# Differential heads: keys and values by seven products over weight sums made in DRAM; the down projection's sums made later

## The chip, the core and the metric

The kernel runs on one core of a Trainium2 chip. TensorE (PE) multiplies, VectorE (DVE), ScalarE (ACT) and GpSimd (POOL) work on tiles in on-chip memory, SyncE (SP) and POOL issue DMAs, which 16 DMA engines carry out. Each engine takes its instructions in program order and waits on semaphores for the others. The metric is device time in microseconds (us), the median of several runs; before the change it is 971.36 us (three runs, 970.71 to 972.44).

## The reference, cut to what matters

One encoder layer on 512 tokens and 16 learned meta tokens (528 rows), model width 1024, in float32. Both attention branches have eight heads.

```
xn = rmsnorm(h)
proj = xn @ w_in                       # sb q|k|v, df q|k|v, 1024 columns each
o_sb = stick-breaking attention, 8 heads of width 128
s = einsum(dq, dk) * 64 ** -0.5        # df: two maps of width 64 per head
p = softmax(where(mask, s - slope * dist, -inf))
w = p[:, :, 0] - lam * p[:, :, 1]
o_df = rmsnorm(w @ dv, subln_g) * (1 - lam_init)
merged = g0 * (o_sb @ w_br_sb) + g1 * (o_df @ w_br_df)   # g = sigmoid(xn @ w_gate + b)
h = h + merged @ w_out
hn = rmsnorm(h)
h = h + (silu(hn @ w_ffn_gate) * (hn @ w_ffn_up)) @ w_ffn_down
y = rmsnorm(h)[16:]
```

## The kernel before

All float32 products are made of two parts: a value is split into a high part (ACT copies it to the PE's fp32r format, `wh`) and a rest (DVE subtracts, `wl`). `mm3` (L259) then issues three matmuls per 128-row slice of the inner dimension: hi*hi, hi*lo, lo*hi (L262, L263, L264). So each weight chunk of 512 KB (1024 x 128, eight slices `k`) goes through: a DMA by SP into a `wst` or `wsu` tile (L179), a cast on ACT and a subtraction on DVE (L77, L78, in `split`), then PE.

The weights come in the order of one list, `stream`. `prepare` runs a given number of chunks ahead of their use and issues loads, casts and splits; the constants STAGE = 5, READY = 3 and, for differential heads and later, 2 set how far.

The program goes: heads of the stick-breaking branch (`br` 0), heads of the differential branch (`br` 1), gates, output projection, feed-forward loop over 22 blocks f of 128 columns, down projection. In a head, PE works on head h's scores and outputs, and in between on `units` of head h+1's q, k and v projections and of the `y` projections of earlier heads; each `yield n` in `sb_head` and `df_head` lets n units run. The 528 rows are two halves of 264 (`HL`), so k and v are made in pieces of 264 columns; `xT_h` and `xT_l` are the split, transposed input.

Stick-breaking heads 2 to 7 make k and v together by seven block products instead of eight (Strassen-Winograd over two halves of the inner dimension, the two weight blocks v and k, and the two token halves). `seven_units` issues them; the weight sums that they need are made on DVE by `c1` to `c4` (L208, L209, L216, L223), the token sums once, in tiles `tA` and `tB`. The feed-forward loop does the same with its gate and up weights (`wst` and `wsu`). Differential heads make k and v plainly: 3 chunks, 8 slices each, `kv_units` for k and the like for v.

In `df_head` (h) DVE reduces the score tiles `z` with the bias to `pr` and their maxima (L676), ACT takes the exponential, DVE scales the two maps and combines them (L705, L706); four tiles t = 0 to 3, of 144 to 528 columns. PE then transposes `pr` (L528), and the outputs follow. `k_evac` splits k (L651, L652) and copies it to the other 64 partitions by a POOL DMA (L655); `q_evac` does it for q (L645). Odd heads keep q and k in a buffer of their own, `dqk`; the row blocks `y_out` of the y projections are added up in DRAM by POOL DMAs (L766, L768).

The down projection also uses seven products. Its weight sums `ds1` to `ds4` (the profile's `ds`) are made in DRAM by POOL DMAs: 24 copies, then 24 accumulating DMAs, 512 KB each but for the last block of each sum (256 KB). `sum_job` (L136 to L141) issues one; each waits for the last cast that ACT had been given, which paces it. Before the change one job is issued after every second unit of the heads, from 16 us to 393 us. After the gates only `hres` (L1044, four POOL DMAs of 512 KB, the residual input) and loads use the DMA engines.

In the gates POOL multiplies each gate by its y (L1036), DVE adds the two (L1037) and ACT casts the sum.

Of the kernel before, what the change touches and what calls it, by code (L numbers as in the profile page):

```python
# [9 lines left out]
F32 = mybir.dt.float32  # L10
# [30 lines left out]
def block_kernel(ctx: ExitStack, tc: tile.TileContext, x, meta, norm_mix_g, w_in, w_gate, b_gate,  # L41
# [46 lines left out]
    for h in range(NH):  # L88

        for i in (0, 1, 2) if h < SEVEN else (2, 1, 0):  # L90
            cols(("sb", h, i), w_in, i * D + h * P)
        if h > 2:
            rows(("y_sb", h - 3), w_br_sb, (h + 1) % 2 * 512, (h - 3) // 2 * 2)
    for h in range(NH):
        for i in range(3):
            cols(("df", h, i), w_in, (3 + i) * D + h * P)
        if h < 3:
            rows(("y_sb", h + 5), w_br_sb, (h + 1) % 2 * 512, (h + 5) // 2 * 2)
        else:
            rows(("y_df", h - 3), w_br_df, (h + 1) % 2 * 512, (h - 3) // 2 * 2)  # L100
# [17 lines left out]
    DK = range(0, NK, 2)  # L118
    sums_dram = ctx.enter_context(tc.tile_pool(name="sums_dram", bufs=1, space=bass.MemoryType.DRAM))
    w_sum = {(n, k0): sums_dram.tile([P, 2, 512], F32, name=f"d{n}_{k0}") for n in ("s1", "s2", "s3", "s4") for k0 in DK}  # L120
# [3 lines left out]
    for w, _, _ in DOWN:  # L124
        for k0 in DK:
# [3 lines left out]
            else:  # L129
                stream.append((("down", w, k0), w_sum[w, k0], 0, 512, 0, min(2, NK - k0)))  # L130

    def raw_down(w, k0):
        k, c0 = raw_at[w]
        return w_fd[:, k + k0:k + min(k0 + 2, NK), c0:c0 + 512]

    def sum_job(to, of, k0, add):  # L136
        src = raw_down(of, k0) if of in raw_at else w_sum[of, k0][:, 0:min(2, NK - k0)]
        dst = w_sum[to, k0][:, 0:min(2, NK - k0)]
        kw = dict(accum_op=ALU.add, max_dma_last_dim=2048) if add else {}
        paced = mybir.DependencyInfo(mybir.DependencyClass.Sync, mybir.DependencyReason.DATA)  # L140
        tc.add_manual_dep(nc.gpsimd.dma_start(dst, src, **kw).ins, cast["last"].ins.name, paced)  # L141

    background = [(to, of, k0, i > 3) for i, (to, of) in enumerate(
        (("s1", "a21"), ("s2", "a11"), ("s3", "a21"), ("s4", "a12"), ("s1", "a22"), ("s3", "a11"), ("s2", "s1"), ("s4", "s2")))
        for k0 in DK]

# [10 lines left out]
    def stage_one():  # L157
        n = len(staged)
        if n == len(stream):
            return False  # L160
        key, view, c0, cw, k0, k1 = stream[n]

        if n >= first_down + 3 and "slots" not in fpools:
            return False
        if key[0] == "fu" and key[1]:
            if "w" not in fpools:
                return False
            st = fpools["w"].tile([P, KT, P], F32, tag="wsu", bufs=2, name="wsu")
# [8 lines left out]
        staged.append(st)  # L177
        for a, b in ((0, 4), (4, 8)) if n < 2 else ((0, k1 - k0),):
            nc.sync.dma_start(st[:, a:b], view[:, k0 + a:k0 + b, c0:c0 + cw])  # L179
        return True  # L180
# [69 lines left out]
    def weights(key):  # L250
        at = at_of[key]
        if at < START:
            return loaded[key]
        if at >= first_ffn:
            return fpools["down"](key)
        prepare(prep_at[key] + (READY if at < at_of["df", 0, 0] else 2))
        return loaded[key]
# [144 lines left out]
    def seven_units(f, vT, k_neg):  # L402
# [5 lines left out]
        def run(w, t, i, start):  # L408
            prepare(prep_at[{"a": c1, "s": c2}[w[0]] if w in ("a11", "a12", "s1", "s2") else c4 if w == "s4" else c3, f] + READY)
            product(f, w, xsum[t], e[i], start)  # L410
# [33 lines left out]
    def kv_all(br, h, k_evac, d):  # L444
        vu, turn = v_units((br, h, 2), d)
        if sevens((br, h, 1)):
            return seven_units((br, h), d["vT"], k_evac), turn
# [180 lines left out]
    def df_units(h):  # L628
        d = {}
        hs = (slice(0, 64), slice(64, 128))  # L630
        if h % 2:

            both = opool.tile([P, 4 * L + 2 * SEQ], F32R, tag="y_df", name="dqk", bufs=1)
            q = [both[:, 4 * L + c * SEQ:4 * L + (c + 1) * SEQ] for c in range(2)]
            k = [both[:, 2 * c * L:2 * (c + 1) * L].rearrange("p (a l) -> p a l", a=2) for c in range(2)]
# [12 lines left out]
        def k_evac(ps, s, scale):  # L648
            for c in range(2):
# [99 lines left out]
    def y_units(name, i, o):  # L749

        def unit(fs):
            wh, wl = weights((name, i))
            for f in fs:
                ps = mm_tile()
                cs = slice(f % 4 * P, (f % 4 + 1) * P)
                mm3(ps, [(wh[:, k, cs], wl[:, k, cs], o[0][:, k], o[1][:, k]) for k in range(2)])
                if y_out:
                    ys = y_out[0][:, y_count[0] % KT]
                elif y_count[0] % 2:
# [268 lines left out]
    for f in range(KT):  # L1028
# [135 lines left out]
    with tc.tile_pool(name="ffn", bufs=1) as fp:  # L1164
# [102 lines left out]
        for f in range(1, NFF):  # L1267
# [152 lines left out]
```

## Time and profile before

| what | value |
|---|---|
| median of three runs | 971.36 us (970.71 to 972.44) |
| the profiled execution | 970.92 us |
| its span, first to last instruction | 969.1 us, granted PE clock 0.998 |
| start | 0 to 56 us |
| stick-breaking heads | 56 to 236 us, 28 us each |
| differential heads | 236 to 494 us, 30.05 us each |
| gates | 494 to 581 us |
| output projection, start of the feed-forward block | 581 to 663 us |
| feed-forward loop | 663 to 870 us, 10.03 us per block f |
| down projection and end | 870 to 969 us |

A row of a stage table (a time window) gives the window, its length, then for each engine the busy time and the number of instructions, the clock that PE was granted, the mean busy share of the 16 DMA engines, and GB/s. A group of instructions reads: line, engine, operation, output<-inputs, shape, count | busy us, mean ns | idle time before, and what ended it. A timeline row has start, duration, engine, line, operation, and in brackets the idle time before with its releaser. A DMA queue's row has packets, MB, and the time that its packets took as a share of 16 engines; q0 is POOL's, q1 is SP's. A load's row ends with KB each and the median us from issue to landing. A wait's row has total us, times, longest.

### The profile page before, as it was taken

The numbers are of one execution on the slowest core, as the hardware profiler recorded it, in microseconds if no ns is written. First come the engines' busy times: TensorE is split into PE (matmuls) and PEld (weight loads), VectorE is DVE, ScalarE is ACT, GpSimd is POOL, SyncE is SP. The second block draws the span as 40 slices with busy tenths as digits, with TensorE's granted clock in tenths as the row PEclk, the third lists the DMA queues.
The fourth block names the chain that finished last, engine by engine and source line by source line (L and its number), as shares of the span: only waits on it lengthen the run. The fifth ranks groups of instructions, "written<-read, shape, count | busy, mean of one in ns | idle before, by whom it ended". The sixth has DMA issues, their size and how long they took to land.

```text
span 969.1 us, 16156 instructions
## 1 busy us (share of the span) xinstructions
PE 948.4 (98%) x6117; PEld 853.8 (88%) x6118; DVE 701.2 (72%) x1292; ACT 588.0 (61%) x1128; POOL 183.8 (19%) x198
## 2 busy tenths in 40 slices
PE   8998999999999999999999999989999999999997
PEld 6997888898899998999878888879999999988886
DVE  7988687766567776678632433699888888989785
ACT  7666766666566666666773433575555555666554
POOL 3201111222353433422315430000000000000013
PEclk9999999999999999999999999999999999999999
DMA  8334656679989989754739733124433334276552
GB/s 242 109 104 126 188 167 176 171 164 208 194 183 189 172 199 198 155 139 111 153 100 259 237 121 100 57 62 134 129 89 111 108 95 123 67 240 205 181 168 87
DMA packets 151439, 145.83 MB, mean 150 GB/s; under 512 B 6049, under 2 KB 116802, under 8 KB 151362
## 3 DMA queue, kind: packets, MB, share of 16 engines
q1 hardware_dynamic: 131794, 97.94, 34.0%
q0 software_dynamic: 19408, 46.80, 23.8%
q8 instruction: 48, 0.79, 0.3%
q14 instruction: 29, 0.24, 0.1%
q10 hardware_dynamic: 160, 0.07, 0.0%
HBM read 121.59 MB, written 41.94 MB: 169 GB/s over the span
## 4 chain that ended last, share of the span: by engine, by line
PE 86%; DVE 6%; ACT 4%; DMA 3%; issue 1%; DVEq 0%; ACTq 0%; SPq 0%
PE mm L264 19%; PE mm L263 19%; PE mm L262 19%; PE z L262 7%; PE z L263 7%; PE z L264 7%; DMA wst<-in_w_in_dram 2%; PE z L673 1%; PE z L672 1%; DVE wl L78 1%; PE tr L528 1%; PE z L528 1%; ACT wh L77 1%; PE tr L504 1%; PE z L556 0%
## 5 line engine op out<-in xcount | busy, mean ns | idle before, releaser
L262 PE MATMUL mm<-xT_h,wh 128*128 128x264 f32 (+2 forms) x656 | 214.3, 327 | 0.5 <-ACT xT_h L865 0.5
L78 DVE TENSOR_TENSOR wl<-wst,wh 128x1024 fp32r<-128x1024 f32 (+1 forms) x146 | 162.3, 1116 | 72.1 <-ACT wh L77 72.0
L263 PE MATMUL mm<-xT_l,wh 128*128 128x264 f32 (+2 forms) x656 | 213.2, 325 | 0.5
L264 PE MATMUL mm<-xT_h,wl 128*128 128x264 f32 (+2 forms) x656 | 212.8, 324 | 0.0
L77 ACT CAST wh<-wst 128x1024 fp32r<-128x1024 f32 (+1 forms) x146 | 140.2, 962 | 103.0 <-PE mm L263 70.0
L263 PEld LDWEIGHTS mm<-xT_l,wh 128*128 128x128 f32 x656 | 123.4, 188 | 10.4 <-DVE xT_l L866 1.3
L262 PEld LDWEIGHTS mm<-xT_h,wh 128*128 128x128 f32 x656 | 123.6, 188 | 10.0 <-ACT xT_h L865 0.9
L264 PEld LDWEIGHTS mm<-xT_h,wl 128*128 128x128 f32 x656 | 123.4, 188 | 9.9
L263 PE MATMUL mm<-hT_l,wh 128*128 128x256 f32 x284 | 80.6, 285 | 0.7 <-DVE hT_l L1107 0.7
L262 PE MATMUL mm<-hT_h,wh 128*128 128x256 f32 x284 | 80.3, 285 | 0.6 <-DVE sg L1202 0.6
L264 PE MATMUL mm<-hT_h,wl 128*128 128x256 f32 x284 | 80.1, 283 | 0.0
L1322 POOL TENSOR_TENSOR outs<-hres,gF 128x512 f32<-128x512 f32 x4 | 7.2, 1799 | 283.2 <-DVE hres L1308 278.1
L141 POOL DMA_DIRECT2D ds<-in_w_ffn_down_dram x36 | 28.5, 791 | 156.0 <-ACT wh L77 106.0
L676 DVE CUSTOM_DVE_ANT_0 pr<-z,bias 128x144 f32<-128x144 f32 (+3 forms) x64 | 30.9, 502 | 35.0 <-PE z L673 34.9
L263 PEld LDWEIGHTS mm<-hT_l,wh 128*128 128x128 f32 x284 | 53.7, 189 | 1.1 <-DVE hT_l L1107 1.1
L262 PEld LDWEIGHTS mm<-hT_h,wh 128*128 128x128 f32 x284 | 53.4, 189 | 1.0 <-DVE sg L1202 0.8
L264 PEld LDWEIGHTS mm<-hT_h,wl 128*128 128x128 f32 x284 | 53.6, 189 | 0.0
L262 PE MATMUL mm<-o_h,wh 128*128 128x512 f32 x128 | 53.1, 415 | 0.0
L262 PE MATMUL z<-wh,da 128*128 128x512 f32 (+1 forms) x132 | 50.9, 386 | 0.3 <-DVE hres L1308 0.3
L264 PE MATMUL mm<-o_h,wl 128*128 128x512 f32 x128 | 50.8, 397 | 0.0
L263 PE MATMUL mm<-o_l,wh 128*128 128x512 f32 x128 | 50.1, 392 | 0.3 <-DVE o_l L744 0.3
L263 PE MATMUL z<-wl,da 128*128 128x512 f32 (+1 forms) x132 | 50.4, 382 | 0.0
(344 smaller groups left out, 2560.1 us busy)
## 6 DMA issues: line engine op xcount, KB each, us to landing
wst<-in_w_in_dram SPq DMA_DIRECT2D x40, 512.0 KB, 7.2
ds<-in_w_ffn_down_dram POOLq DMA_DIRECT2D x30, 512.0 KB, 5.1
wst<-in_w_ffn_gate_dram SPq DMA_DIRECT2D x22, 512.0 KB, 3.8
wsu<-in_w_ffn_up_dram SPq DMA_DIRECT2D x21, 512.0 KB, 3.8
y_df<-y_out POOLq DMA_DIRECT2D x32, 256.0 KB, 5.7
wst<-in_w_gate_dram SPq DMA_DIRECT2D x16, 512.0 KB, 5.9
slots<-ds SPq DMA_DIRECT2D x13, 512.0 KB, 3.3
ds<-ds POOLq DMA_DIRECT2D x10, 512.0 KB, 8.1
```

The costliest lines, as they stand in the source:

```text
L77: cast["last"] = (hi_copy or nc.scalar.copy)(hi, src)
L78: (lo_eng or nc.vector).tensor_tensor(lo, src, hi.bitcast(F32), op=ALU.subtract)
L141: tc.add_manual_dep(nc.gpsimd.dma_start(dst, src, **kw).ins, cast["last"].ins.name, paced)
L262: nc.tensor.matmul(ps, lhsT=ah, rhs=bh, start=(start and i == 0), stop=False, skip_group_check=skip)
L263: nc.tensor.matmul(ps, lhsT=ah, rhs=bl, start=False, stop=False, skip_group_check=skip)
L264: nc.tensor.matmul(ps, lhsT=al, rhs=bh, start=False, stop=(stop and i == n - 1), skip_group_check=skip)
L504: nc.tensor.transpose(pt[:, j * P:(j + 1) * P], vT[:, j * P:(j + 1) * P], ident)
L528: nc.tensor.transpose(pt[:, (t - j) * P:(t - j + 1) * P], blocks(t, j * P, (j + 1) * P), ident)
L672: nc.tensor.matmul(o, lhsT=q[c][:, qs], rhs=k[c][:, 0, k0:k1], start=True, stop=False)
L673: nc.tensor.matmul(o, lhsT=q[c][:, qs], rhs=k[c][:, 1, k0:k1], start=False, stop=True)
L676: nc.vector.tensor_tensor_reduce(po, zz, bb, scale=1.0, scalar=-3.0e38, op0=ALU.add, op1=ALU.max, accum_out=mx[:, t, c:c + 1])
L1322: nc.gpsimd.tensor_tensor(outs[t][:, D1], hres[:, t, D1], gF[:, D1], op=ALU.mult)
```

## The change

Differential heads make k and v by `seven_units` too. The sums of their weights don't come from DVE: for each group of four heads two tiles in DRAM, `s21` and `s34`, are filled by POOL DMAs, 16 jobs per group (8 copies, 8 accumulates, 512 KB each), which are put ahead of the down projection's 48 jobs. A head then loads four chunks for k and v: `a` (v's raw weights), `b` (s21), `c` (half of s34 and half of k's raw weights, two DMAs) and `d` (the other half of s34, half a chunk), and q's chunk last. q's units now run after those of k and v. One set of q and k tiles serves all heads, since the token sums tA and tB stay where `dqk` and `y_out` were; `y_out` has four rows in tiles `s21` and `wsu` of the heads' pool, and eight rows, `y_last`, for the last head. k's copy across partitions is issued when its first half is made, which now comes last.

Jobs are issued by `tick`: three per five units in the stick-breaking heads (all 32 k and v jobs, and the first job of the down projection at the change of branch), none in the differential heads, one after each of the 24 gate units of f > 1, three per step of the feed-forward loop until none is left.

```diff
@@ the list of chunks
     for h in range(NH):
-        for i in range(3):
-            cols(("df", h, i), w_in, (3 + i) * D + h * P)
+        s21, s34, c0 = kv_sum[h // 4]["s21"], kv_sum[h // 4]["s34"], h % 4 * P
+        cols(("df", h, "a"), w_in, 5 * D + h * P)
+        cols(("df", h, "b"), s21, c0)
+        stream.append((("df", h, "c"), [(s34, c0, 0, 4), (w_in, 4 * D + h * P, 4, 8)], 0, P, 0, KT))
+        stream.append((("df", h, "d"), s34, c0, P, 4, KT))
+        cols(("df", h, 0), w_in, 3 * D + h * P)
...
-    background = [(to, of, k0, i > 3) for i, (to, of) in enumerate(
-        (("s1", "a21"), ("s2", "a11"), ("s3", "a21"), ("s4", "a12"), ("s1", "a22"), ("s3", "a11"), ("s2", "s1"), ("s4", "s2")))
-        for k0 in DK]
...
+    def sum_jobs(raw, kept, ks):
+        return [lambda to=to, of=of, k0=k0, i=i: summed_in(kept(to, k0), (raw if of[0] == "a" else kept)(of, k0), i > 3)
+                for i, (to, of) in enumerate((("s1", "a21"), ("s2", "a11"), ("s3", "a21"), ("s4", "a12"),
+                                              ("s1", "a22"), ("s3", "a11"), ("s2", "s1"), ("s4", "s2")))
+                for k0 in ks]
...
+    background = sum(([*sum_jobs(raw_kv(g), kept_kv(g), (0, 2))] for g in range(2)), [])
+    background += sum_jobs(raw_down, lambda w, k0: w_sum[w, k0][:, 0:min(2, NK - k0)], DK)
+    ticks = [0]
+
+    def tick(num=1, den=2):
+        ticks[0] += 1
+        if background and ticks[0] * num // den > (ticks[0] - 1) * num // den:
+            background.pop(0)()
@@ weights
-        prepare(prep_at[key] + (READY if at < at_of["df", 0, 0] else 2))
+        prepare(prep_at[key] + (READY if at < at_of["df", 0, "a"] or key[0] == "df" else 2))
@@ seven_units
+            if f[0] == "df":
+                n, k = {"a11": ("a", K1), "a12": ("a", K2), "s2": ("b", K1), "s1": ("b", K2), "s3": ("c", K1), "a22": ("c", K2),
+                        "s4": ("d", K1)}[w]
+                wh, wl = weights(f + (n,))
+                ops[f, w] = wh[:, k], wl[:, k]
@@ kv_all
-        if sevens((br, h, 1)):
+        if br == "df" or sevens((br, h, 1)):
@@ df_units
-        if h % 2:
...
-        else:
-            q = [ap_.tile([P, SEQ], F32R, tag=("qh", "ql")[c], name=f"dq{c}") for c in range(2)]
-            k = [ap_.tile([P, 2, L], F32R, tag=("kh", "kl")[c], name=f"dk{c}") for c in range(2)]
+        q = [ap_.tile([P, SEQ], F32R, tag=("qh", "ql")[c], name=f"dq{c}") for c in range(2)]
+        k = [ap_.tile([P, 2, L], F32R, tag=("kh", "kl")[c], name=f"dk{c}") for c in range(2)]
...
-                if s.stop == L:
+                if s.start == 0:
                     nc.gpsimd.dma_start(k[c][hs[1 - c]].bitcast(F32), k[c][a].bitcast(F32))
...
-        return d, halves(("df", h, 0), xT, QT, q_evac) + kv, turn
+        return d, kv + halves(("df", h, 0), xT, QT, q_evac), turn
@@ the heads' loop
-            y_out.append(xtp.tile([P, KT, SEQ], F32, tag="y_sb", name="y_out"))
+            y_out += [v[:, i] for v in [ap_.tile([P, 2, SEQ], F32, tag=t, name="y_out") for t in ("s21", "wsu")] for i in range(2)]
...
-                    if background and unit_count[0] % 2 == 0:
-                        sum_job(*background.pop(0))
+                    if br == 0 or len(background) > 8 * len(DK):
+                        tick(3, 5)
@@ gates
                 for u in gate(br, f, sg[br], AF.Sigmoid):
                     u()
+                    tick(1, 1)
@@ feed-forward loop, at the end of a step
+            for _ in range(3):
+                tick(1, 1)
```

VectorE in a differential head, from the reductions of tile 3 on: this is before the change (`dqk` are the next head's q and k, `nm` and `rc` are small statistics).

```order
L706 SCALAR_TENSOR_TENSOR pr<-pr,rc 128x400
L652 SCALAR_TENSOR_TENSOR dqk<-mm,dqk 64x264
L698 TENSOR_SCALAR nm<-mx 128x2
L78 TENSOR_TENSOR wl<-wst,wh 128x1024
L652 SCALAR_TENSOR_TENSOR dqk<-mm,dqk 64x264
L703 RECIPROCAL rc<-ls 128x2
L704 TENSOR_TENSOR rc<-rc,cn 128x2
L652 SCALAR_TENSOR_TENSOR dqk<-mm,dqk 64x264
L705 TENSOR_SCALAR pr<-pr,rc 128x528
L706 SCALAR_TENSOR_TENSOR pr<-pr,rc 128x528
L78 TENSOR_TENSOR wl<-wst,wh 128x1024
```

The same place of the changed kernel, where L688 is k's split, L681 q's, L482 v's second half and L742 the last step of `pr`.

```order
L742 SCALAR_TENSOR_TENSOR pr<-pr,rc 128x400
L688 SCALAR_TENSOR_TENSOR dk_5267<-mm,dk_5267 64x264
L482 TENSOR_TENSOR vT<-mm,qq 128x264
L734 TENSOR_SCALAR nm<-mx 128x2
L78 TENSOR_TENSOR wl<-wst,wh 128x1024
L688 SCALAR_TENSOR_TENSOR dk_5268<-mm,dk_5268 64x264
L78 TENSOR_TENSOR wl<-wst,wh 128x1024
L739 RECIPROCAL rc<-ls 128x2
L740 TENSOR_TENSOR rc<-rc,cn 128x2
L741 TENSOR_SCALAR pr<-pr,rc 128x528
L742 SCALAR_TENSOR_TENSOR pr<-pr,rc 128x528
L78 TENSOR_TENSOR wl<-wst,wh 128x1024
```

A second weight split and a sum into vT now stand ahead of the last `pr`; q's splits, which stood earlier in the stretch, come after it.

GpSimd's queue from the last gates to the end, before the change (`gF` is a gain that the end needs):

```order
L1036 TENSOR_TENSOR sg<-sg,y_sb 128x512
L1036 TENSOR_TENSOR sg<-sg,y_df 128x512
L1167 DMA gF<-in_norm_final_g_dram 128x1024
L1322 TENSOR_TENSOR outs<-hres,gF 128x512 x2
L1323 TENSOR_TENSOR outs<-hres,gF 128x512 x2
```

And the same stretch of the changed kernel, the first rows from the gates, the last from the feed-forward loop (L1074 is the product, L140 a job of the sums):

```order
L1074 TENSOR_TENSOR sg<-sg,y_sb 128x512
L140 DMA ds_4_100<-in_w_ffn_down_dram 256x1x512
L140 DMA ds_6_101<-in_w_ffn_down_dram 256x1x512
L1074 TENSOR_TENSOR sg<-sg,y_df 128x512
L140 DMA ds_8_102<-in_w_ffn_down_dram 256x1x512
L140 DMA ds_10_103<-in_w_ffn_down_dram 128x512
L1074 TENSOR_TENSOR sg<-sg,y_sb 128x512
L140 DMA ds_0_80<-in_w_ffn_down_dram 256x1x512
L1074 TENSOR_TENSOR sg<-sg,y_df 128x512
```

```order
L1205 DMA gF<-in_norm_final_g_dram 128x1024
L140 DMA ds_2_81<-in_w_ffn_down_dram 256x1x512
L140 DMA ds_4_82<-in_w_ffn_down_dram 256x1x512
L140 DMA ds_6_83<-in_w_ffn_down_dram 256x1x512
L140 DMA ds_8_84<-in_w_ffn_down_dram 256x1x512
L140 DMA ds_10_85<-in_w_ffn_down_dram 128x512
L140 DMA ds_0_92<-in_w_ffn_down_dram 256x1x512
```

Copies stand between the gates' products, and 23 accumulates follow `gF` with no other work of POOL between them; the first of each three waits for a cast of ACT in the loop, so that they go out three together.

More of the change, by code (lines that the diff above doesn't have):

```diff
@@ L93, in block_kernel @@
             rows(("y_sb", h - 3), w_br_sb, (h + 1) % 2 * 512, (h - 3) // 2 * 2)
+    sums_dram = ctx.enter_context(tc.tile_pool(name="sums_dram", bufs=1, space=bass.MemoryType.DRAM))
+    kv_sum = [{n: sums_dram.tile([P, 8, 512], F32, name=f"kv{g}_{n}") for n in ("s21", "s34")} for g in range(2)]
     for h in range(NH):
-        for i in range(3):
-            cols(("df", h, i), w_in, (3 + i) * D + h * P)
+        s21, s34, c0 = kv_sum[h // 4]["s21"], kv_sum[h // 4]["s34"], h % 4 * P
[4 more added lines that the diff above has]
+        cols(("df", h, 0), w_in, 3 * D + h * P)
         if h < 3:
@@ L118, in block_kernel @@
     DK = range(0, NK, 2)
-    sums_dram = ctx.enter_context(tc.tile_pool(name="sums_dram", bufs=1, space=bass.MemoryType.DRAM))
     w_sum = {(n, k0): sums_dram.tile([P, 2, 512], F32, name=f"d{n}_{k0}") for n in ("s1", "s2", "s3", "s4") for k0 in DK}
@@ L130, in block_kernel, with summed_in @@
                 stream.append((("down", w, k0), w_sum[w, k0], 0, 512, 0, min(2, NK - k0)))
+    def summed_in(dst, src, add):
+        kw = dict(accum_op=ALU.add, max_dma_last_dim=2048) if add else {}
+        paced = mybir.DependencyInfo(mybir.DependencyClass.Sync, mybir.DependencyReason.DATA)
+        tc.add_manual_dep(nc.gpsimd.dma_start(dst, src, **kw).ins, cast["last"].ins.name, paced)
+    def sum_jobs(raw, kept, ks):
[3 more added lines that the diff above has]
+                for k0 in ks]
     def raw_down(w, k0):
@@ L134, in raw_down, with raw_kv, raw, kept_kv @@
         return w_fd[:, k + k0:k + min(k0 + 2, NK), c0:c0 + 512]
[L136 to L141, printed above, removed]
-    background = [(to, of, k0, i > 3) for i, (to, of) in enumerate(
-        (("s1", "a21"), ("s2", "a11"), ("s3", "a21"), ("s4", "a12"), ("s1", "a22"), ("s3", "a11"), ("s2", "s1"), ("s4", "s2")))
-        for k0 in DK]
+    def raw_kv(g):
+        at = {"a11": (0, 5), "a12": (4, 5), "a21": (0, 4), "a22": (4, 4)}
+        def raw(w, k0):
+            k, i = at[w]
+            return w_in[:, k + k0:k + k0 + 2, i * D + g * 512:i * D + (g + 1) * 512]
+        return raw
+    def kept_kv(g):
+        at = {"s2": ("s21", 0), "s1": ("s21", 4), "s3": ("s34", 0), "s4": ("s34", 4)}
+        def kept(w, k0):
+            n, k = at[w]
+            return kv_sum[g][n][:, k + k0:k + k0 + 2]
+        return kept
+    background = sum(([*sum_jobs(raw_kv(g), kept_kv(g), (0, 2))] for g in range(2)), [])
[5 more added lines that the diff above has]
+            background.pop(0)()
     at_of = {c[0]: n for n, c in enumerate(stream)}
@@ L177, in stage_one @@
         staged.append(st)
+        if isinstance(view, list):
+            for v, c, a, b in view:
+                nc.sync.dma_start(st[:, a:b], v[:, a:b, c:c + cw])
+            return True
         for a, b in ((0, 4), (4, 8)) if n < 2 else ((0, k1 - k0),):
@@ L408, in run @@
         def run(w, t, i, start):
-            prepare(prep_at[{"a": c1, "s": c2}[w[0]] if w in ("a11", "a12", "s1", "s2") else c4 if w == "s4" else c3, f] + READY)
+            if f[0] == "df":
[3 more added lines that the diff above has]
+                ops[f, w] = wh[:, k], wl[:, k]
+            else:
+                prepare(prep_at[{"a": c1, "s": c2}[w[0]] if w in ("a11", "a12", "s1", "s2") else c4 if w == "s4" else c3, f] + READY)
             product(f, w, xsum[t], e[i], start)
@@ L630, in df_units @@
         hs = (slice(0, 64), slice(64, 128))
-        if h % 2:
-            both = opool.tile([P, 4 * L + 2 * SEQ], F32R, tag="y_df", name="dqk", bufs=1)
-            q = [both[:, 4 * L + c * SEQ:4 * L + (c + 1) * SEQ] for c in range(2)]
-            k = [both[:, 2 * c * L:2 * (c + 1) * L].rearrange("p (a l) -> p a l", a=2) for c in range(2)]
-        else:
-            q = [ap_.tile([P, SEQ], F32R, tag=("qh", "ql")[c], name=f"dq{c}") for c in range(2)]
-            k = [ap_.tile([P, 2, L], F32R, tag=("kh", "kl")[c], name=f"dk{c}") for c in range(2)]
+        q = [ap_.tile([P, SEQ], F32R, tag=("qh", "ql")[c], name=f"dq{c}") for c in range(2)]
+        k = [ap_.tile([P, 2, L], F32R, tag=("kh", "kl")[c], name=f"dk{c}") for c in range(2)]
         d["q"], d["k"] = q, k
@@ L756, in unit @@
                 mm3(ps, [(wh[:, k, cs], wl[:, k, cs], o[0][:, k], o[1][:, k]) for k in range(2)])
-                if y_out:
-                    ys = y_out[0][:, y_count[0] % KT]
+                if y_out and (len(y_out) > 4 or y_count[0] % 8 > 3):
+                    ys = y_out[y_count[0] % len(y_out)]
                 elif y_count[0] % 2:
@@ L960, in block_kernel @@
     turn()
-    todo, unit_count = [], [0]
+    todo = []
     for br in range(2):
@@ L982, in block_kernel @@
             if turn is None:
+                y_last = opool.tile([P, KT, SEQ], F32, tag="y_df", name="y_last", bufs=1)
+                y_out[:] = [y_last[:, i] for i in range(KT)]
                 sg0 = [gate_tile(br) for br in range(2)]
@@ L992, in block_kernel @@
                     units.pop(0)()
-                    unit_count[0] += 1
-                    if background and unit_count[0] % 2 == 0:
-                        sum_job(*background.pop(0))
+                    if br == 0 or len(background) > 8 * len(DK):
+                        tick(3, 5)
             for u in units:
@@ L1279, in block_kernel @@
             ready(at_job(c4, f) + 2)
+            for _ in range(3):
+                tick(1, 1)
+        assert not background
         tp_ctx.close()
```

## The prediction

> **What bounds the kernel now.** I read the page first: busy shares, then the chain that ended last.
>
> ```profile
> PE 948.4 (98%) x6117; PEld 853.8 (88%) x6118; DVE 701.2 (72%) x1292; ACT 588.0 (61%) x1128; POOL 183.8 (19%) x198
> PE 86%; DVE 6%; ACT 4%; DMA 3%; issue 1%; DVEq 0%; ACTq 0%; SPq 0%
> ```
>
> TensorE is busy for 98% of the span and carries 86% of the chain, so a removed matmul is worth its pitch wherever nothing else is about to be late. The question is where something is. So I read the table by stages: differential heads (254 to 464), gates (536 to 584), feed-forward loop (693 to 703), and the change of branch (226 to 254).
>
> ```profile
> core 0: us, PE busy (x) PEld busy (x) DVE busy (x) ACT busy (x) POOL busy (x), PEclk, DMA share, GB/s
> 198.00:226.00 28.00, 28.00 (x185) 25.04 (x184) 18.01 (x27) 18.66 (x35) 7.62 (x10) 1.00 0.78 178
> 226.00:254.00 28.00, 26.47 (x182) 23.92 (x182) 16.19 (x23) 16.47 (x31) 7.64 (x10) 1.00 0.96 195
> 284.00:314.00 30.00, 30.00 (x200) 27.45 (x199) 21.09 (x55) 19.84 (x47) 12.77 (x13) 1.00 1.00 195
> 434.00:464.00 30.00, 30.00 (x201) 27.47 (x199) 21.09 (x55) 19.85 (x47) 8.78 (x9) 1.00 0.57 125
> 500.00:536.00 36.00, 35.72 (x157) 29.14 (x156) 12.03 (x14) 16.98 (x26) 16.82 (x18) 1.00 0.94 242
> 560.00:584.00 24.00, 24.00 (x108) 19.87 (x107) 8.60 (x10) 8.65 (x12) 7.58 (x5) 1.00 0.35 118
> 693.00:703.00 10.00, 10.00 (x86) 10.00 (x85) 8.53 (x14) 5.53 (x9) 0.00 (x0) 1.00 0.36 105
> ```
>
> PE never stops in heads, gates or feed-forward loop; the DMA engines are nearly full in the first heads (share 1.00) and two thirds empty in the loop (0.36). The change takes matmuls from the heads and moves DMA work into gates and loop.
>
> **Differential heads: matmuls removed, DVE work added.** Per head 12 of 96 matmuls of 264 columns go.
>
> ```profile
> 446.04 0.28 PE L262 MATMUL mm<-xT_h,wh 128*128 128x264 f32 x1
> 446.16 0.28 PE L263 MATMUL mm<-xT_l,wh 128*128 128x264 f32 x1
> 436.80 0.28 PE L672 MATMUL z<-dk,dq 128*128 128x256 f32 x1
> 437.57 0.31 DVE L676 CUSTOM_DVE_ANT_0 pr<-z,bias 128x144 f32<-128x144 f32 x1 [4.47 <-PE z L673]
> 455.63 0.77 DVE L706 SCALAR_TENSOR_TENSOR pr<-pr,rc 128x528 f32<-128x528 f32 x1
> 457.00 0.93 PE L528 MATMUL tr<-ident,pr 128*128 128x128 f32 x7
> 466.84 0.28 PE L672 MATMUL z<-dqk 128*128 128x256 f32 x1
> ```
>
> Starts are 0.12 us apart, so 12 x 0.12 = 1.44 us per head, 11.5 us for eight: the whole gain. A head lasts 466.84 - 436.80 = 30.04 us. Inside it DVE runs from the first reduction (437.57) to the last probability (455.63 + 0.77 = 456.40), 18.83 us, and PE's transposes begin at 457.00: only 0.6 us of slack. All units of the next head's projections stand before the transposes, so the whole 1.44 us are taken out of PE's side of this race, while DVE's side grows:
>
> ```profile
> L78 DVE TENSOR_TENSOR wl<-wst,wh 128x1024 fp32r<-128x1024 f32 x28 | 34.3, 1223 | 13.6 <-ACT wh L77 13.6
> L645 DVE SCALAR_TENSOR_TENSOR dqk<-mm,dqk 64x512 fp32r<-64x512 f32 x8 | 5.5, 689 | 0.2
> L652 DVE SCALAR_TENSOR_TENSOR dqk<-mm,dqk 64x264 fp32r<-64x264 f32 x16 | 6.9, 430 | 0.6
> 698.88 0.68 DVE L78 TENSOR_TENSOR wl<-wst,wh 128x512 fp32r<-128x512 f32 x1
> ```
>
> In that stretch the order has 4 weight splits and a half one in place of 3 (+1.22 + 0.68), two sums into vT and one into qq (three 264-column operations, priced by dk's 0.43: +1.29), and the two q evacuations go behind the transposes (-2 x 0.69). Net +1.8 us. DVE's rows in the stretch hold 1.0 us of idle time that can take some of it, so DVE needs 19.6 (idle all used) to 20.6 us (none). From transposes to the next scores are 9.84 us, from scores to the first reduction 0.77: a head of 30.2 to 31.2 us by DVE's loop against 28.6 by PE's. A reduction that starts a little earlier (the first score matmul moves up) or a split put later takes the low end to 29.4. From the pure PE gain to the worst walk that is -1.44 to +1.15 us per head, -10 to +8 for the seven full ones. I take the row it is nearest to, DVE's own loop at about 30.0: **0**. The 1.44 us become a wait of PE for `pr`. k's cross-partition copy hides behind the scores of the old head (landing 5 us, needed some 20 us later); without that cover it would cost its 5. q and k keep one buffer instead of two: q's evacuation now waits for the old head's scores, which are done before the transposes behind which it stands, 9 us before it is needed, so I cost it at 0. The y rows keep fewer buffers too, in the scheme that the stick-breaking heads use, where PE has no gap (198 to 226: 28.00 of 28); also 0.
>
> **Change of branch.** Here the 226 to 254 row has 1.5 us of PE idle at a DMA share of 0.96, and loads queue:
>
> ```profile
> q0 software_dynamic: 1368, 2.71, 79.0%
> q1 hardware_dynamic: 1607, 1.18, 23.3%
> wst<-in_w_in_dram SPq DMA_DIRECT2D x3, 512.0 KB, 17.6
> ```
>
> (217 to 236 us.) The first differential head now needs 4.5 chunks instead of 3, from sums that POOL has just written. -1.4 (PE's gain in that head) to +6; I take **+1**.
>
> **Stick-breaking heads.** Jobs come 3 per 5 units instead of 1 per 2, with accumulates among them. The up loads are just in time already:
>
> ```profile
> DVE s L208 <- DMA wsu<-in_w_in_dram: 8.5, 5, 3.3
> ```
>
> 0 to +3, **+1**.
>
> **Gates.** The copies of the down sums, 24 of them, now lie here, one after each gate unit.
>
> ```profile
> q0 software_dynamic: 144, 0.52, 20.7%
> 528.94 1.12 POOL L1044 DMA_DIRECT2D hres<-in_x_dram  x2 [5.51 <-DMA y_df<-y_out]
> ```
>
> One copy took 20.7% of 8 us (180 to 188) = 1.65 us of all engines; 24 take 40 us, less than that with the half-size ones. Free in 500 to 584 are 36 x 0.06 + 24 x 0.65 = 18 us in the two quoted rows and some 7 us between them; the hres loads (4 x 1.8) leave, and with them POOL's 5.5 us wait. So the copies nearly fill the stage, and the POOL products of a gate stand behind copies in POOL's queue, as DVE's sum and ACT's next cast stand behind the products. 0 to +8, **+2**.
>
> **Feed-forward loop.** Three accumulates per step f, f = 1 to 8, 23 in all (four of half size), where no POOL DMA ran.
>
> ```profile
> q0 software_dynamic: 1737, 4.03, 69.6%
> ds<-ds POOLq DMA_DIRECT2D x4, 512.0 KB, 7.2
> wst<-in_w_in_dram SPq DMA_DIRECT2D x3, 512.0 KB, 9.1
> q0 software_dynamic: 706, 1.53, 32.5%
> q1 hardware_dynamic: 4880, 2.46, 38.4%
> ```
>
> Window 360 to 390 has four accumulates and the same other POOL transfers as 404 to 434, which has none: (0.696 - 0.325) x 30 = 11.1 us, 2.8 us of all engines each. The last row is 690 to 712: 38.4% of 22 us for 4.7 loads, 1.8 us each. Per step the DMA engines are then asked for 3 x 2.8 + 2 x 1.8 = 12 us in a cycle of 10.03:
>
> ```profile
> 697.19 0.37 SPq L179 DMA_DIRECT2D wsu<-in_w_ffn_up_dram  x1
> 707.22 0.37 SPq L179 DMA_DIRECT2D wsu<-in_w_ffn_up_dram  x1
> wsu<-in_w_ffn_up_dram SPq DMA_DIRECT2D x2, 512.0 KB, 3.6
> 700.57 1.05 ACT L77 CAST wh<-s 128x1024 fp32r<-128x1024 f32 x1 [0.89 <-PE z L263]
> 700.86 0.69 DVE L208 TENSOR_TENSOR s<-wsu 128x512 f32<-128x512 f32 x1 [0.36 <-DMA wsu<-in_w_ffn_up_dram]
> 702.19 1.22 DVE L78 TENSOR_TENSOR wl<-s,wh 128x1024 fp32r<-128x1024 f32 x1
> 704.99 0.28 PE L264 MATMUL mm<-t_h,wl 128*128 128x256 f32 x1
> wst<-in_w_in_dram SPq DMA_DIRECT2D x40, 512.0 KB, 7.2
> ```
>
> The up load lands 3.6 us after its issue and DVE is already waiting for it (0.36 us). Its sum L208 stands in DVE's queue ahead of the split `wl<-s` of the step before, ready at 702.19 + 1.22 = 703.41, which PE needs at 704.99: 1.58 us of slack. A landing beyond 3.6 + 1.5 = 5.1 us stops PE, and the cycle is 10.03 - 5.1 = 4.9 us plus the landing. A burst is released by the cast that ends at 701.62, 5.6 us before the next up load; of its 8.4 us at least 2.8 are left then, more after POOL's issues and the gate load. With equal shares the load lands after 1.8 + 2 x 1.8 = 5.4 us (+0.3 per step, +2 in all), in a queue like that of 360 to 390, where loads landed after 9.1, it costs 4 per step (+31). I take the page's median for 512 KB loads beside background work, 7.2: +2.1 per step, x 23/3 = 16, less 1 for the half-size jobs: **+15**.
>
> [...]
>
> **Sum.** Span 969.1, the profiled run 970.92 us (the median of the runs is 971.36, 0.05% above). 970.92 + 0 + 1 + 1 + 2 + 15 = **990**.
>
> **Rivals.**
> (A) Faster: PE's pace holds. If ACT and DVE use the idle time around the added splits so that `pr` is ready when the transposes come, seven heads give 10 us back; if the burst is over before the up load is served (landing under 5.1), the loop costs 0 to 2. 970.9 - 10 + 2 = 963, at best 970.9 - 11.5 = 959.4. For it: DVE is idle for 9 of 30 us per head. Against: that idle time lies mostly after the transposes, and the demand of 12 us per 10. It decides at 0.6 us of slack and at 5.1 us of landing.
> (B) The bursts hide, the heads don't: DVE paces the heads (0), the loop pays +2, the rest 0 to +4: 971 to 977, or 967 where half of the heads' gain is kept.
> (C) Loads starve as at 217 to 236 and stay so: +4 per step, +31, and the gates +5: 1005 to 1012.
>
> **How the numbers follow.** Forecast (978 to 1004) 0.54, A 0.18, B 0.18, C 0.10. A measurement here tells 0.2%, 2 us: faster is below 969.4. Of B 0.03 is faster, 0.06 the same, 0.09 slower. Faster 0.21, same 0.06, slower 0.73. The range 963 to 1007 leaves out half of A and most of C. Forecast alone: 978 to 1004.
>
> **What would show it.** Heads: the distance of the transposes' starts (30.0 now; 28.6 if the gain is whole), and a wait of L528's matmuls on DVE's `pr`. Loop: steps 1 to 8 longer than 10.03 and later ones equal to it; landings of wsu above 5.1; waits of L208 on wsu (11.7 us in all now) growing. Gates: waits of POOL's product on its own queue and a step above 5.5 us. I am wrong if wsu lands in under 5 us throughout, or if DVE's stretch stays within 18 us.

## The result and the profile after

The changed kernel takes 1025.09 us (median of four runs, 1019.78 to 1027.03) against 971.18 before: 1.0544 times as long, 95% interval 1.0504 to 1.0585. Forecast were 990 us, 978 to 1004, and a range with the rivals up to 1007. The direction was right, the size was not. The page's busy shares, its chain and POOL's queue, after:

```profile
PE 959.5 (94%) x6021; PEld 854.5 (84%) x6022; DVE 723.0 (71%) x1332; ACT 604.0 (59%) x1152; POOL 211.0 (21%) x230
PE 59%; DVE 19%; DMA 12%; ACT 6%; issue 3%; SPq 0%; DVEq 0%; ACTq 0%
q0 software_dynamic: 26064, 63.58, 30.1%
```

PE had carried 86% of the chain; now DVE and the DMA engines carry 31%. PE issues 96 matmuls fewer and is busy 11 us longer. To see where, I cut both traces at the same instructions of PE: the first transposes of each head's probabilities (L528, after the change L570), the first matmul on `hT_l` (feed-forward block), and the last into `z` on `da` (end of the down projection).

| stage (us) | before | after | difference | forecast |
|---|---|---|---|---|
| stick-breaking heads 0 to 7 | 193.6 | 216.5 | +22.9 | +1 |
| change of branch | 34.0 | 42.5 | +8.5 | +1 |
| differential heads 0 to 7 | 206.9 | 207.2 | +0.3 | 0 |
| gates, output projection | 140.9 | 140.9 | 0.0 | +2 |
| feed-forward block, down projection | 336.6 | 358.5 | +21.9 | +15 |

The table by windows of the changed kernel has the same in its PE and clock columns (two bad stretches of the stick-breaking heads, the change of branch, the differential heads, the gates, the loop's start and its later steps):

```profile
84.00:112.00 28.00, 23.34 (x137) 20.98 (x138) 14.84 (x24) 12.74 (x25) 1.61 (x2) 0.86 0.58 121
140.00:170.00 30.00, 22.51 (x138) 19.94 (x137) 14.12 (x31) 14.62 (x31) 4.84 (x7) 0.83 0.61 159
260.00:290.00 30.00, 20.07 (x103) 16.51 (x103) 14.39 (x23) 12.18 (x26) 6.48 (x9) 0.89 0.78 170
350.00:380.00 30.00, 29.67 (x190) 26.16 (x189) 23.55 (x64) 22.10 (x51) 8.33 (x11) 1.00 0.61 150
560.00:590.00 30.00, 30.00 (x134) 24.87 (x133) 12.49 (x11) 9.19 (x12) 16.09 (x17) 1.00 1.05 356
700.00:715.00 15.00, 7.11 (x49) 6.92 (x48) 8.00 (x13) 4.10 (x8) 1.74 (x3) 0.77 0.86 193
790.00:805.00 15.00, 15.00 (x128) 15.00 (x127) 12.89 (x21) 8.46 (x14) 0.00 (x0) 1.00 0.41 120
```

A mean DMA share tells little: the gates run at 1.05 without a gap of PE, the window from 84 to 112 loses 4.7 us at 0.58. What counts is what stands just ahead of one load. The timeline of that head (POOL, SP, DVE, PE in turn), and the load's row:

```profile
79.64 0.69 POOL L140 DMA_DIRECT2D kv_s<-in_w_in_dram  x1 [8.83 <-ACT wh L77]
81.56 0.69 POOL L140 DMA_DIRECT2D kv_s<-in_w_in_dram  x1 [1.23 <-ACT kh L618]
82.79 1.20 POOL L140 DMA_DIRECT2D kv_s<-in_w_in_dram  x1 [0.55 <-ACT wh L77]
83.68 0.37 SPq L215 DMA_DIRECT2D wsu<-in_w_in_dram  x1
94.11 0.69 DVE L244 TENSOR_TENSOR s<-wsu 128x512 f32<-128x512 f32 x1 [6.23 <-DMA wsu<-in_w_in_dram]
95.58 0.59 PE L298 MATMUL z<-kh,qh 128*128 128x264 f32 x1 [4.11 <-DVE o_l L667]
95.96 0.42 PE L299 MATMUL z<-kl,qh 128*128 128x264 f32 x1
96.18 0.42 PE L300 MATMUL z<-kh,ql 128*128 128x264 f32 x1
wsu<-in_w_in_dram SPq DMA_DIRECT2D x1, 512.0 KB, 10.3
```

Three copies go out within 3.2 us, then the up load is issued and lands after 10.3 us. DVE, in order, stands 6.23 us before L244, and `o_l` of the old head is queued behind it; PE stands 4.11 us. Then its matmuls start 0.22 us apart, not 0.12, until 98.8: the granted clock of that window is 0.86.

The second loss, 38.2 us for the head around 150, has a cause of 32 KB:

```profile
152.94 0.29 DVE L829 TENSOR_TENSOR lp<-lam 128x128 f32<-128x128 f32 x1 [8.70 <-DMA lam<-in_lam_k_dram]
154.94 0.77 PE L598 MATMUL z<-a_s,vf 128*128 128x128 f32 x2 [7.49 <-DVE a_s L589]
lam<-in_lam_k_dram SPq DMA_DIRECT2D x2, 32.0 KB, 11.5
```

The lambda vectors, loaded in the fifth head, landed after 5 us before the change and DVE did not wait for them; here they are issued from 138.0 to 141.0, behind two weight loads and two accumulates and just ahead of a third, and DVE waits 8.70 us with the head's work behind it.

These two heads lose 8.3 and 10.3 us. The other 4.3 of the 22.9 lie between the last two transposes of the branch (232 to 266), where ACT waits for chunk `b` of the first differential head:

```profile
237.67 1.05 ACT L77 CAST wh<-wst 128x1024 fp32r<-128x1024 f32 x1 [3.38 <-DMA wst<-kv_s]
```

At the change of branch ACT waits for chunk `c` of the second differential head, made ready ahead of its use; the second half of that chunk, raw weights, landed 12.5 us after its issue (first row below). In the feed-forward loop DVE waits for the up load:

```profile
266.07 0.50 SPq L212 DMA_DIRECT2D wst<-in_w_in_dram  x1
278.73 1.04 ACT L77 CAST wh<-wst 128x1024 fp32r<-128x1024 f32 x1 [9.20 <-DMA wst<-in_w_in_dram]
282.39 0.79 PE L298 MATMUL z<-a_h,vh 128*128 128x512 f32 x1 [7.93 <-DVE a_l L573]
706.29 0.69 DVE L244 TENSOR_TENSOR s<-wsu 128x512 f32<-128x512 f32 x1 [10.52 <-DMA wsu<-in_w_ffn_up_dram]
710.27 0.58 PE L298 MATMUL mm<-hT_h,wh 128*128 128x256 f32 x1 [7.89 <-ACT qx L1248]
DVE s L244 <- DMA wsu<-in_w_ffn_up_dram: 37.3, 19, 10.5
```

The waits on the up load grew from 11.7 to 37.3 us. The first was the worst: its load was issued at 688.54 and landed after 17.7 us. Three accumulates had been issued just ahead of it, from 685.4, and three more from 694.5, while it was under way. POOL had stood 70.4 us behind `gF`, so that the first group went out at once when `gF` did.

### The profile page after: what moved, and what is told of

It reads as the page before. It is cut to its first block, busy times and chain, and to the rows that moved or that the text cites. A ratio compares the mean times of both kernels' runs of the same rounds, so it can differ in the third digit from the quotient of the medians.

```text
span 1023.2 us, 16134 instructions
## 1 busy us (share of the span) xinstructions
PE 959.5 (94%) x6021; PEld 854.5 (84%) x6022; DVE 723.0 (71%) x1332; ACT 604.0 (59%) x1152; POOL 211.0 (21%) x230
## 4 chain that ended last, share of the span: by engine, by line
PE 59%; DVE 19%; DMA 12%; ACT 6%; issue 3%; SPq 0%; DVEq 0%; ACTq 0%
PE mm L298 12%; PE mm L300 12%; PE mm L299 12%; DVE wl L78 6%; PE z L298 6%; PE z L299 6%; PE z L300 6%; DMA wsu<-in_w_ffn_up_dram 5%; DMA wsu<-in_w_in_dram 2%; ACT wh L77 2%; DMA wst<-in_w_in_dram 1%; DVE s L653 1%; DMA lam<-in_lam_k_dram 1%; DVE pr L712 1%; ACT pr L736 1%
## 5 line engine op out<-in xcount | busy, mean ns | idle before, releaser
L78 DVE TENSOR_TENSOR wl<-wst,wh 128x1024 fp32r<-128x1024 f32 (+1 forms) x162 | 181.0, 1120 | 75.1 <-ACT wh L77 74.9
L77 ACT CAST wh<-wst 128x1024 fp32r<-128x1024 f32 (+1 forms) x162 | 153.0, 948 | 104.6 <-PE mm L299 45.1
L298 PE MATMUL mm<-xT_h,wh 128*128 128x512 f32 (+2 forms) x496 | 169.8, 342 | 0.9 <-ACT xT_h L901 0.5
L299 PE MATMUL mm<-xT_l,wh 128*128 128x512 f32 (+2 forms) x496 | 168.6, 340 | 0.5
L300 PE MATMUL mm<-xT_h,wl 128*128 128x512 f32 (+2 forms) x496 | 167.0, 339 | 0.0
L298 PEld LDWEIGHTS mm<-xT_h,wh 128*128 128x128 f32 x496 | 94.1, 190 | 10.4 <-ACT xT_h L901 0.9
L299 PEld LDWEIGHTS mm<-xT_l,wh 128*128 128x128 f32 x496 | 93.9, 189 | 10.5 <-DVE xT_l L902 1.3
L300 PEld LDWEIGHTS mm<-xT_h,wl 128*128 128x128 f32 x496 | 93.4, 189 | 9.6
L244 DVE TENSOR_TENSOR s<-wsu 128x512 f32<-128x512 f32 x27 | 18.7, 691 | 55.0 <-DMA wsu<-in_w_ffn_up_dram 37.3
L712 DVE CUSTOM_DVE_ANT_0 pr<-z,bias 128x144 f32<-128x144 f32 (+3 forms) x64 | 30.5, 502 | 29.0 <-PE z L709 28.9
```

The costliest lines, as they stand in the source:

```text
L77: cast["last"] = (hi_copy or nc.scalar.copy)(hi, src)
L78: (lo_eng or nc.vector).tensor_tensor(lo, src, hi.bitcast(F32), op=ALU.subtract)
L244: nc.vector.tensor_tensor(s[:, K2], u[:, K1], u[:, K2], op=ALU.add)
L298: nc.tensor.matmul(ps, lhsT=ah, rhs=bh, start=(start and i == 0), stop=False, skip_group_check=skip)
L299: nc.tensor.matmul(ps, lhsT=ah, rhs=bl, start=False, stop=False, skip_group_check=skip)
L300: nc.tensor.matmul(ps, lhsT=al, rhs=bh, start=False, stop=(stop and i == n - 1), skip_group_check=skip)
```

## The experiments

Theory: the jobs of the sums cost what the loads cost that they hold up, in three places, and the differential heads gain nothing for a reason of their own. The rivals stand with each run. "Heads" are the distances of the transposes, as in the table.

**No jobs for k and v.**

```diff
-        cols(("df", h, "b"), s21, c0)
+        cols(("df", h, "b"), w_in, 4 * D + h * P)
... (the same for chunks c and d)
-    background = sum(([*sum_jobs(raw_kv(g), kept_kv(g), (0, 2))] for g in range(2)), [])
-    background += sum_jobs(
+    background = sum_jobs(
... (no ticks in the heads)
```

> Leaves out the 32 sum jobs for k and v: the differential heads read raw weights in the places of the sums (same bytes, same chunks), the rest is the changed kernel; the 48 down jobs all run in gates and feed-forward loop. Theory (the jobs of the k and v sums delay loads in the stick-breaking heads, +22.5 us, and at the change of branch, +8.5 us): both go, about 994 us, heads of 28 us again and PE clock near 0.99. Rival 1 (the change of branch is slow because a differential head now loads 4.5 chunks instead of 3): 1002 us, the 8.5 us stay. Rival 2 (PE's lower granted clock, 0.977, is a cause of its own and no consequence of PE's gaps): the clock stays near 0.977 and the time above 1005 us.

Measured: 990.58 us (two runs), PE clock 0.992. Stick-breaking heads 191.4, change of branch 34.6, differential heads 207.3, feed-forward block +19.2 against before. The 32 jobs cost 34.5 us in all, 25 in the heads and 8 at the change of branch, which rival 1 had kept: 4.5 chunks in 34.6 us are no burden without jobs beside them. The clock came back with the gaps gone, against rival 2.

**Only the seven products are left.** The same kernel with `tick(1, 2)` in all heads and no ticks in gates and loop.

> The kernel of the run before, with the down sums' 48 jobs back in the heads, one per two units as before the change, none in gates and feed-forward loop: only the seven products of the differential heads are left of the change, with raw weights in the place of the sums. Theory (a head is paced by VectorE's loop at 29.8 us, so the 1.44 us of matmuls saved per head are nearly all lost): 969 to 972 us. Rival 1 (VectorE's pace came from the late loads around it, and PE sets the pace when the queues are quiet): heads of 28.6 us, 960 us. Rival 2 (4.5 + 1 chunks per head beside background jobs are too much for the DMA engines): heads of 31 us or more, 980 us.

Measured: 985.48 us (980.50 to 993.13, four runs). All three expectations missed. The heads without an accident took 29.5 to 30.5 us, but the change of branch took 40.5, and one head waited for k's copy across partitions:

```profile
382.89 0.55 PE L707 MATMUL z<-dk,dq 128*128 128x256 f32 x1 [4.33 <-DMA dk<-dk]
```

So the down sums, which cost about 2 us in the heads before the change (the run "down sums late" below), cost 13 us beside the new heads: 6.4 at the change of branch, 6.6 in the differential heads.

**One accumulate per step.** `for _ in range(2 if f < 4 else 1)` in place of `range(3)`.

> The changed kernel with one accumulate per step of the feed-forward loop (two in the first three steps) instead of three in each of the first eight. Theory (a burst of three, 8.4 us of the DMA engines, holds up the next up load; one of 2.8 us is over before it): steps of 10.03 us from the fourth on, 1003 to 1007 us in all. Rival (any accumulate in flight holds up the load, and their number counts, not their grouping): each of 20 steps 1 us longer, 1022 us or more.

Measured: 1009.21 us (two runs), 2 us above the theory's range and far from the rival's. The feed-forward block is 5.0 us above before instead of 21.9; 3.5 of the 5.0 come in the first two steps with jobs, the later steps take 10.03. Waits of L244 on the up load fall from 37.3 to 17.4 us. The grouping counts, not the number.

**Lambda vectors loaded at the start.**

```diff
-        lam4 = opool.tile([P, 4, 64], F32, tag="sg1", name="lam4")
+    lam4 = ap_.tile([P, 4, 64], F32, name="lam4")
```

(with its four loads, at the start of the program)

> The changed kernel with the four small loads of the lambda vectors issued at the start of the program instead of in the fifth stick-breaking head. Theory (VectorE stood 8.7 us for these 32 KB behind weight loads and accumulates, and that is the head of 38.2 us): that head falls to 28 to 29 us, 1015 us in all. Rival (the weight loads in the same queue are as late, so that the next wait takes its place): the head stays above 34 us, 1021 us or more.

Measured: 1017.00 us (two runs). That head took 29.05 us in place of 38.24, as the theory says; the whole time is 2 us above its 1015.

**The kernel before, down sums late.** 24 copies behind gate units, three accumulates per step, nothing else.

> The kernel before, with only the down sums' jobs moved as the change moves them: 24 copies behind the gate units, the accumulates three per step of the feed-forward loop; differential heads as before. Theory (the bursts alone hold up the up loads of the loop): loop 19 to 22 us longer, gates the same, 2 us less in the stick-breaking heads that lose their jobs, 988 to 992 us. Rival (the loop suffers only behind the changed heads, through buffers or queue lanes that they leave occupied): below 978 us.

Measured: 992.23 us (two runs), at the upper end of the theory, feed-forward block +23.0 us, gates 0, stick-breaking heads -2.2, waits on the up load 38.4 us. The loss in the feed-forward block is the move of these jobs alone.

**Two weight splits on GpSimd.**

```diff
+        on_pool = n < 3 or at_of["df", 0, "a"] <= n < at_of["gate", 0, 0] and (key[0][0] == "y" or key[2] == "d")
-        split(wh, wl, staged[n], nc.gpsimd if n < 3 else None)
+        split(wh, wl, staged[n], nc.gpsimd if on_pool else None)
```

> The first run's kernel (raw weights in the place of the k and v sums, no jobs for them) with one accumulate per step of the loop, and with GpSimd in VectorE's place for the lower parts of two weight chunks of each differential head, the half chunk d and the y chunk (1.9 us of VectorE's time per head). Theory (VectorE's loop paces the head at 29.8 us): heads of 28.6 to 29.0 us, 967 to 971 us; without that effect it would be 976. Rival (the head is paced by something else, or GpSimd's splits are late): heads of 29.7 us or more, 975 us or more.

Measured: 992.89 us (two runs), heads of 32.7 to 33.1 us: 3 us longer, not 1 shorter. The groups of one VectorE operation from 340 to 400, first in this run, then in the run without k and v jobs, and POOL's split of the y chunk:

```profile
L742 DVE TENSOR_SCALAR pr<-pr,rc 128x400 f32<-128x400 f32 x2 | 4.9, 2462 | 0.1
392.15 2.37 POOL L78 TENSOR_TENSOR wl<-wst,wh 128x1024 fp32r<-128x1024 f32 x1 [7.45 <-ACT wh L77]
```

```profile
L740 DVE TENSOR_SCALAR pr<-pr,rc 128x400 f32<-128x400 f32 x2 | 0.9, 429 | 0.1
```

An operation of 0.43 us takes 2.46 us, about the 2.37 us that POOL's split lasts. The run doesn't test the theory; it gave VectorE a new wait. The next one does.

**The same two splits left out.** `cast["last"] = nc.scalar.copy(wh, staged[n])` and `loaded[key] = (wh, wh)` for these chunks.

> The first run's kernel with one accumulate per step of the loop, as in the run with the splits on GpSimd, but here the lower parts of chunk d and of the y chunk of the differential heads are left out: PE multiplies with the high parts in their place, the same matmuls, 1.9 us less for VectorE per head and nothing more for GpSimd. Theory (VectorE's loop paces the head): heads of 28.6 to 28.9 us, 967 to 971 us. Rival (something else paces it, and the GpSimd run showed no more than GpSimd being slow): heads of 29.5 us or more, 975 us or more.

Measured: 974.01 us (eight runs, 969.74 to 979.32), heads of 29.43 us. Between theory and rival, nearer to the rival. PE's wait for `pr` between the transposes, 0.5 us, is gone, and the next wait stands right behind it (ACT, then PE, of one head):

```profile
361.53 0.59 ACT L684 ACTIVATE dq<-mm 64x512 fp32r<-64x512 f32 x1
362.03 0.94 ACT L576 CAST a_h<-tr 128x512 fp32r<-128x512 f32 x2
362.65 0.50 PE L302 MATMUL z<-a_h,vh 128*128 128x512 f32 x1
363.54 0.39 PE L712 MATMUL z<-dk,dq 128*128 128x256 f32 x1 [0.39 <-DVE dq L685]
```

The output matmul on `a_h` is 0.89 us from its successor (0.32 before the change): q's evacuation, moved behind k and v, now stands in ACT's queue ahead of `a_h` and in DVE's ahead of the next scores.

**Half the rate.** `tick(1, 2)` for `tick(3, 5)`, with the early lambda loads.

> The run with the early lambda loads, with k's and v's sum jobs one per two units instead of three per five. Theory (at three per five units three copies went out within 4 us, just ahead of an up load, and the head from 76 to 110 us paid 8 us for it): that head falls to 26 or 27 us as before the change, the change of branch stays above 40 us, 1008 to 1011 us in all. Rival (the rate doesn't matter, each job costs): that head stays above 32 us, 1015 us or more.

Measured: 1007.94 us (two runs). The head after 76 us took 27.3 us (33.8 in the run with early lambda loads alone): two copies instead of three ahead of its up load, which landed after 5.4 us instead of 10.1. The change of branch stayed at 44.3.

**Jobs spread.** First group's jobs 1 per 3 units, the second group's in the differential heads, 2 per 3, one accumulate per step, early lambda loads.

> The whole change, computed in full, with its jobs spread: early lambda loads; in the stick-breaking heads only the first group's 16 jobs, one per three units; the second group's 16 in the first differential heads, two per three units; down sums in the gates and one accumulate per step of the loop. Theory (jobs cost what loads they hold up, not their number): stick-breaking heads within 3 us of before, change of branch 35 to 37 us, differential heads 30 to 30.5 while jobs run and 29.8 after, loop +5: 976 to 983 us. Rival (jobs in the differential heads cost as in the run with the down sums there): 985 us or more.

Measured: 988.84 us (two runs), the rival. Part of the second group's sums were read by a head's load ahead of their last additions here, which also held POOL up for 11.6 us; k's copy came behind them, and the third head waited 6.30 us for it. Where no job ran, at the change of branch, it took 34.8 us.

**Jobs paused at the change of branch.** `if len(background) > 8 * len(DK) and (br or h < 7): tick(1 + br, 2 + br)`, three ticks in the output projection, one per step.

> The whole change with early lambda loads and its jobs laid elsewhere: k and v sums one per two units in the stick-breaking heads 0 to 6, none in head 7, the rest two per three units in the first differential heads; three accumulates in the output projection and one per step of the loop. Theory (what counts is the load that a job delays): stick-breaking heads +3 us against before, change of branch 36 to 40 us, the first two differential heads 30 to 31 us, loop +3: 978 to 985 us. Rival (the copy of k across partitions is late again behind the accumulates, 5 to 6 us): 986 us or more.

Measured: 983.25 us (980.01 to 985.72, three runs), the time as expected: stick-breaking heads +1.4, change of branch +0.8, differential heads +7.3, feed-forward block +2.1. The first differential head missed its 30 to 31 us: it took 35.8, since a weight chunk issued among two copies and two accumulates landed after 18.8 us, and ACT waited 5.18 for it; k's copy, the rival's reason, was not waited for. The best full version of the change that I ran is still 1.1% above the kernel before.

**Scaling on ScalarE.**

```diff
+                if t < 3:
+                    nc.scalar.activation(pr[:, 0], pr[:, 0], AF.Copy, scale=rc[:, 0:1])
```

> The kernel of the run before with the scaling of the first map moved from VectorE to ScalarE for tiles 0 to 2 (1.1 us of VectorE's time per differential head). Theory (VectorE's loop paces the head): heads near 29.0 us, 5 us less than the run before. Rival (the extra hand-over between engines delays the last probabilities as much): the same time as the run before, within 2 us.

Measured: 991.92 us (986.40 to 995.29, three runs), heads of 30.15 us in place of 29.78. The rival, and worse: in the heads one hand-over more per tile costs more than the time that it frees on VectorE. That explains about 2 us; the profile, taken at 986.40, is 3 us above the run before, and the rest of the 8.7 between the medians stays unexplained.

## Why the prediction was wrong, step by step

- **Differential heads, 0 for the gain of 11.5 us: right in size, in part by luck.** Measured +0.3, which is two things. The first six distances fell by 1.8 us together (from 30.04 to 29.8 each, the first to 29.5). The last one grew by 2.1: there are no k and v of a next head to save there, but PE waits for `a_h` and `dq` behind the late q (last two rows below). The mechanism was half right. I gave the whole loss to VectorE's loop, with a stretch that grows from 18.83 to 19.6 or more and a head of 30.2. VectorE's work in the stretch did grow by the 1.81 us that I had added up, but the stretch took 18.88 us (first two rows below): 0.8 us went into idle time and about 1.0 into overlap, since an operation's row starts before the one ahead of it ends (a split `wl` lasts from 443.41 to 444.64 us, the step of `pr` behind it starts at 444.56). PE's transposes now start 0.8 us before the stretch ends, and the later ones wait for `pr` in six of the eight heads (third and fourth row):

```profile
439.04 0.31 DVE L712 CUSTOM_DVE_ANT_0 pr<-z,bias 128x144 f32<-128x144 f32 x1 [4.14 <-PE z L709]
457.15 0.77 DVE L742 SCALAR_TENSOR_TENSOR pr<-pr,rc 128x528 f32<-128x528 f32 x1
457.09 0.60 PE L570 MATMUL tr<-ident,pr 128*128 128x128 f32 x4
457.98 0.55 PE L570 MATMUL tr<-ident,pr 128*128 128x128 f32 x3 [0.28 <-DVE pr L742]
490.39 0.50 PE L298 MATMUL z<-a_h,vh 128*128 128x512 f32 x1 [0.68 <-ACT a_h L572]
491.28 0.39 PE L708 MATMUL z<-dk,dq 128*128 128x256 f32 x1 [0.40 <-DVE dq L681]
```

  With 1.9 us less for VectorE only 0.35 us came back. Of the 1.44 us saved, PE's start-to-start distances in one head show 0.5 lost between the transposes, 0.3 at the first score, which waits for q, 0.3 in output and `y` matmuls that start a little further apart, and 0.1 in the seven products themselves; I had costed the later q at nothing, as done "9 us before it is needed".
- **Stick-breaking heads, +1 (0 to +3): the step that failed.** The text said "the up loads are just in time already", and then bounded the cost by the waits of before, as though the rate of jobs alone changed. What matters is how many jobs stand ahead of one load. Three copies instead of two nearly doubled that load's landing (10.1 against 5.4 us), and the lambda loads, which I did not list at all, cost 9. Measured +22.9; the run without the jobs shows that they are the whole of it (-2.2 against before).
- **Change of branch, +1 (-1.4 to +6): right place, half of the reason, price too low.** I named 4.5 chunks instead of 3. Without jobs they cost 0.6 us (34.6 against 34.0), and jobs beside 3 chunks cost nothing (34.0 before the change, 33.9 without them). The two together cost 6.4 with the down sums (40.5) and 8.5 here.
- **Gates, +2 (0 to +8): 0.** The DMA engines ran at 1.05 there and the 24 jobs, 23 copies and an accumulate, fitted.
- **Feed-forward loop, +15 (+2 to +31): right mechanism, size 7 us short.** Bursts hold up the up load, steps without them keep their time (10.0 us from one L244 to the next, 794 to 884), and one accumulate per step nearly hides (waits on the up load of 37.3 us with three, 17.4 with one, 11.7 before). My 7.2 us landing was a median over loads beside single jobs; the landings here alternate between 4 to 5 and 8 to 9 us after a first one of 17.7. While both queues had work, from 694 to 704, POOL's (q0) and SP's (q1) moved packets one for one, but SP's carried a quarter of the bytes:

```profile
q0 software_dynamic: 872, 1.67, 89.8%
q1 hardware_dynamic: 871, 0.45, 21.9%
```

  At this rate, 87 packets a us, the 1040 packets of a load (2080 for two loads from 693 to 703 before the change) would take about 12 us, an estimate, as long as POOL's jobs last; alone it lands after 3.6 to 4.0.
- **Left out: what a gap costs after it ends.** Up to PE's last matmul at 1016 us the granted clock of the changed kernel is at one half in eight stretches of 3.4 to 10.2 us, each around the end of a gap of PE: all seven gaps of 2.79 to 7.93 us are among them, and one of 1.99; after the other gaps, of 1.69 us or less, it stays at 1.00. For 3 to 7 us after such a gap PE's matmuls start nearly twice as far apart (0.22 us in place of 0.12 at 264 columns). Adding up the excess of these distances gives 10 to 15 us of the 54, an estimate that depends on which matmuls are counted. No term of my sum had it: before the change PE had no gap above 1.53 us in these stages, and the clock stayed at 1.00.
- **Rivals.** C named 217 to 236 as the pattern, loads starving beside POOL's queue; that is what came, and it had 0.10, with the stick-breaking heads not among its places, so that its 1005 to 1012 us were too low as well. A fell: where the queues are quiet the heads take 29.8 us all the same.

Open stays whether the 1.44 us per head can be had at all: with q's units between v and k and fewer splits it was not tried.

## What to carry to other kernels

A background transfer's price here was not its bytes but the one load that it stood ahead of. List every load that some engine waits for in order, the smallest too, with its slack; then ask how many jobs can leave between its predecessor and it when they are released together, and space them so that one fits into the slack. A saving in a stage where one engine is at 100% and the next has 0.6 us of slack is worth no more than that at first (here 0.25 of 1.44 us came back), so sum the work added to the second one, and to what is moved behind it, before counting matmuls. And each of the seven stops of PE of 2.79 to 7.93 us cost more than it lasted in this kernel, and so did one of 1.99.

## What the runs showed of the hardware that was not expected

- The clock after gaps: 0.22 us between 264-column matmuls in place of 0.12 for 3.3 us after a gap of 4.1 us, 0.43 between 512-column ones in place of 0.23 for 5 us after one of 7.5. A gap's length alone does not decide. The same gap of 1.99 us, at the same place of the program, was followed by a granted clock of 0.50 in the changed kernel (81.85 to 88.65, first row) and of 1.00 in the run with early lambda loads (80.80 to 87.00, second row); the same four transposes took 1.12 and 0.66 us:

```profile
81.86 1.12 PE L570 MATMUL z<-ident,s 128*128 128x128 f32 x4 [1.99 <-DVE a_l L573]
```

```profile
80.80 0.66 PE L570 MATMUL z<-ident,s 128*128 128x128 f32 x4 [1.99 <-DVE a_l L573]
```

  Four half-clock stretches of the changed kernel last 3.41 us (gaps of 2.79 to 4.11 us), three 6.83 (gaps of 1.99, 7.89 and 7.93) and one 10.24 (a gap of 7.49). What sets these lengths was not shown.
- A VectorE operation beside a GpSimd subtraction of 2.37 us: the `TENSOR_SCALAR` from `pr` to `pr` with 400 columns took 2.46 us in the run with the splits on GpSimd, 0.43 in the run without k and v jobs. The reductions of 144 columns from `z` that ran beside the same splits kept their 0.30 us.
